# A new order of 36 transfers, and eleven instead of seven pairs of x tiles transposed on VectorE

## The chip, the cores and the metric

The kernel runs on one core of one Trainium2 chip. The metric is device microseconds of one execution. A profiled execution also has a *span*, from the first to the last instruction, some 2 us shorter than the time. Most executions of the kernel before agree within 0.3%. In the lines of the profile PE is TensorE, DVE is VectorE, ACT is ScalarE, and SPq is the sequencer that issues all transfers.

## The reference

```python
# x (16, 512, 1024), weight (1024, 768), sub_value (16, 512, 768), all float32
def reference(x, weight, sub_value):
    return (np.matmul(x, weight) - sub_value).astype(np.float32)
```

The rows of x form 64 tiles of 128 rows ("tile 0" to "tile 63"). x is 33.6 MB, the weight 3.1, sub_value and the output 25.2 each: 87.0 MB that any kernel has to move.

## The kernel before

Each x tile is cast to float16 on ScalarE. It is then transposed, either on TensorE (PE: four transposes and a copy on ScalarE) or, in pairs of tiles listed in `ON_DVE`, on VectorE. PE multiplies, and VectorE subtracts sub_value from the product in PSUM, the memory into which PE writes. One queue issues all transfers in the order of a list; `(kind, first tile, count)`.

```python
ON_DVE = frozenset(range(18, 60, 6))          # 7 pairs
TRANSFERS = [
    ('x', 0, 1), ('w', 0, 1), ('x', 1, 1), ('w', 1, 1), ('x', 2, 1), ('w', 2, 1),
    ('w', 3, 1), ('x', 3, 2), ('s', 0, 1), ('x', 5, 3), ('s', 1, 3), ('x', 8, 3),
    ('s', 4, 4), ('x', 11, 5), ('s', 8, 8), ('x', 16, 8), ('x', 24, 3), ('s', 16, 8),
    ('x', 27, 5), ('o', 0, 8), ('s', 24, 8), ('x', 32, 8), ('s', 32, 8), ('o', 8, 8),
    ...
]
```

x lives in a ring of 16 tiles, sub and out share a ring of 32. A transfer is not issued before its ring slots are free, and nothing behind it in the list is issued before it:

```python
need, by = {
    "w": (set(), "o"),
    "x": ({t for t in old if t >= 0}, "cast"),    # tiles 16 back are cast
    "s": ({t for t in old if t >= 0}, "o"),       # outputs 32 back are written
    "o": (span, "finish"),                        # these tiles are subtracted
}[kind]
if not need <= done[by]:
    return
```

Inside an iteration of the main loop (tile `mi`), PE multiplies tile `mi` with the transposes of tile `mi + 2` in between; then come the casts of tiles ahead (4 ahead for PE's tiles, 7 for VectorE's), the subtraction, and four of the 16 transposes of a pair on VectorE.

Of the kernel before, what the change touches and what calls it, by code (L numbers as in the profile page):

```python
# [17 lines left out]
LEAD_DVE = 7  # L18
PER = 4
HEAD = 3  # L20
ON_DVE = frozenset(range(18, 60, 6))

TRANSFERS = [
    ('x', 0, 1), ('w', 0, 1), ('x', 1, 1), ('w', 1, 1), ('x', 2, 1), ('w', 2, 1),
    ('w', 3, 1), ('x', 3, 2), ('s', 0, 1), ('x', 5, 3), ('s', 1, 3), ('x', 8, 3),
    ('s', 4, 4), ('x', 11, 5), ('s', 8, 8), ('x', 16, 8), ('x', 24, 3), ('s', 16, 8),
    ('x', 27, 5), ('o', 0, 8), ('s', 24, 8), ('x', 32, 8), ('s', 32, 8), ('o', 8, 8),
    ('x', 40, 8), ('s', 40, 8), ('x', 48, 8), ('o', 16, 8), ('o', 24, 8), ('s', 48, 8),
    ('x', 56, 8), ('s', 56, 8), ('o', 32, 8), ('o', 40, 8), ('o', 48, 8), ('o', 56, 4),
    ('o', 60, 2), ('o', 62, 1), ('o', 63, 1),  # L30
]


# [1 line left out]
def kernel(  # L35
# [88 lines left out]
    def cast(mi):  # L124
        assert mi in done["x"]
        done["cast"].add(mi)
        x_in = x_ring[:, mi % NX]
        first = mi - mi % 2
        if first in ON_DVE:
            if mi == first:  # L130
                x16_t["pair", mi] = x16p_pool.tile([P, 2, K], F16, name="x16p_tile")
            keep(nc.scalar.copy(out=x16_t["pair", first][:, mi - first], in_=x_in))  # L132
        else:
            x16_t[mi] = x16_pool.tile([P, K], F16, name="x16_tile")
            keep(nc.scalar.copy(out=x16_t[mi], in_=x_in))  # L135
        issue()


    def transposes(mi):
        def one(c):  # L140
            def f():
                if c == 0:
                    ps_t[mi] = psum_t_pool.tile([P, K], F16, name="psum_t")
                keep(nc.tensor.transpose(  # L144
                    ps_t[mi].bitcast(F32)[:, c * P : (c + 1) * P],
                    x16_t[mi].bitcast(F32)[:, c * P : (c + 1) * P],
                    ident,
                ))
                if c == n_c - 1:
                    xt_t[mi] = xt_pool.tile([P, K], F16, name="xt_tile")  # L150
                    keep(nc.scalar.copy(out=xt_t[mi], in_=ps_t.pop(mi)))  # L151
                    x16_t.pop(mi)
            return f
        return [one(c) for c in range(n_c)]

    def transposes_dve(mi):

        x16 = x16_t.pop(("pair", mi)).bitcast(F32).rearrange("p j (c q) -> p (j c) q", c=n_c)
        xt_p = xtp_pool.tile([P, 2, K], F16, name="xtp_tile")
        xt_t[mi], xt_t[mi + 1] = xt_p[:, 0], xt_p[:, 1]  # L160
        xt = xt_p.bitcast(F32).rearrange("p j (c m) -> p (j c) m", c=n_c)

        def one(a, b):
            def f():
                keep(nc.vector.transpose(  # L165
                    xt[b * Q : (b + 1) * Q, :, a * Q : (a + 1) * Q],
                    x16[a * Q : (a + 1) * Q, :, b * Q : (b + 1) * Q],
                ))
            return f
        return [one(a, b) for a in range(P // Q) for b in range(P // Q)]  # L170
# [14 lines left out]
    def finish(mi):  # L185
        assert mi in done["s"]
        done["finish"].add(mi)
        o = so_ring[:, mi % NSO].rearrange("p (h n) -> p h n", h=2)
        keep(nc.vector.tensor_tensor(  # L189
            out=o, in0=po_t.pop(mi)[:, :, :NS], in1=o, op=mybir.AluOpType.subtract  # L190
        ))
        issue()
# [10 lines left out]
    def idle(n):  # L203
        for _ in range(n):
            keep(nc.tensor.matmul(idle_o[:, 0], idle_w, idle_x, start=True, stop=True))  # L205

    def lead(mi):
        return LEAD_DVE if mi - mi % 2 in ON_DVE else TA + CA

# [1 line left out]
        for f in transposes(mi):  # L211
            f()

    idle(13)
    cast(0)
    transpose_tile(0)
    idle(5)
# [28 lines left out]
    for mi in range(HEAD, n_mt):  # L246
        t = mi + TA
        tr = transposes(t) if t < n_mt and t - t % 2 not in ON_DVE else []
        for c in range(n_c):
# [6 lines left out]
        finish(mi)  # L256
        if mi + LEAD_DVE - 1 in ON_DVE:
            waiting += transposes_dve(mi + LEAD_DVE - 1)
# [34 lines left out]
```

## Time and profile before

| | before |
|---|---|
| time, median of the first three runs | 211.42 us |
| span of the profiled run | 209.4 us |
| DMA queue, share of 16 engines' span | 97.7% |
| PE / VectorE / ScalarE busy | 198.4 / 114.1 / 112.6 us |
| last subtraction starts | 204.5 us |

The lines that carry these stand in the prediction. One more view: the queue's own issues in order of time (start, length, what, count).

```profile
78.97 0.33 SPq L122 DMA_DIRECT2D x_ring<-in_x_dram  x1
80.94 0.33 SPq L122 DMA_DIRECT2D so_ring<-in_sub_value_dram  x1
81.32 0.42 SPq L120 DMA_DIRECT2D out_dram<-so_ring  x1
```

The first line is the issue of x 32-39. At that moment the end of outputs 0-7 and all of sub 24-31 were still queued ahead of it.

### The profile page before, as it was taken

What the parts mean: (1) busy time and instruction counts of PE and PEld (TensorE: products, weight loads), DVE (VectorE), ACT (ScalarE), POOL (GpSimd) and SP (SyncE); (2) the same over time, 40 slices, a digit from 0 to 9 for tenths busy, and PEclk for the clock granted to TensorE, in tenths of its full rate; (3) what the DMA queues carried; (4) which work ended last, traced back from release to release, by engine and by line L of the source; (5) the groups of instructions that cost most, each with busy time, mean ns of one, the idle gap of its engine ahead of it and who ended that gap; (6) DMA issues with size and microseconds to landing.
All of it is one profiled execution on the core that took longest, in us unless ns stands there. A gap on an engine that the chain in (4) does not pass through costs nothing.

```text
span 209.4 us, 2967 instructions
## 1 busy us (share of the span) xinstructions
PE 198.4 (95%) x1249; PEld 130.4 (62%) x1249; DVE 114.1 (54%) x186; ACT 112.6 (54%) x115; POOL 0.7 (0%) x6
## 2 busy tenths in 40 slices
PE   7998789999979999999999999999999999999990
PEld 2464467676656576676666666667666766766660
DVE  0342044206149849929946965992994795332231
ACT  3555565675396183655727629355573760765410
POOL 1000000000000000000000000000000000000000
PEclk9999999999999999999999999999999999999999
DMA  6999999999999999999999999999999999999994
GB/s 221 420 426 424 424 438 439 433 443 426 391 455 415 442 427 423 454 413 432 435 421 449 423 413 444 451 418 421 418 441 440 423 437 418 426 446 427 415 383 167
DMA packets 5629, 87.22 MB, mean 417 GB/s; under 512 B 624, under 2 KB 624, under 8 KB 2032
## 3 DMA queue, kind: packets, MB, share of 16 engines
q1 hardware_dynamic: 5616, 87.03, 97.7%
q8 instruction: 10, 0.16, 0.3%
q14 instruction: 3, 0.02, 0.0%
HBM read 61.87 MB, written 25.17 MB: 416 GB/s over the span
## 4 chain that ended last, share of the span: by engine, by line
PE 68%; DMA 20%; ACT 4%; DVE 3%; SPq 1%; issue 1%
PE psum_o L177 60%; DMA x_ring<-in_x_dram 20%; PE psum_t L144 8%; ACT x_tile L135 2%; DVE xtp_tile L165 2%; ACT xt_tile L151 1%; DVE so_ring L189 1%; SPq L110 1%; SPq L122 1%; ACT x16p_tile L132 0%
## 5 line engine op out<-in xcount | busy, mean ns | idle before, releaser
L177 PE MATMUL psum_o<-w_sb,xt_tile 128*128 128x384 f16 x800 | 145.7, 326 | 1.7 <-ACT xt_tile L151 1.1
L177 PEld LDWEIGHTS <-xt_tile 128*128 128x128 f16 x800 | 78.2, 98 | 41.5 <-ACT xt_tile L151 1.9
L189 DVE TENSOR_TENSOR so_ring<-psum_o,so_ring 128x768 f32<-128x768 f32 x64 | 60.7, 957 | 61.2 <-PE psum_o L177 41.1
L151 ACT COPY xt_tile<-psum_t 128x1024 f16<-128x1024 f16 x50 | 50.6, 1012 | 75.7 <-PE psum_t L144 74.9
L165 DVE STREAM_TRANSPOSE xtp_tile<-x16p_tile 32x256 f32<-32x256 f32 x112 | 48.8, 436 | 18.9 <-ACT x16p_tile L132 17.2
L144 PE MATMUL psum_t<-ident,x_tile 128*128 128x128 f32 x200 | 52.5, 275 | 2.8 <-ACT x_tile L135 2.4
L135 ACT CAST x_tile<-x_ring 128x1024 f16<-128x1024 f32 x50 | 51.6, 1049 | 5.5 <-DMA x_ring<-in_x_dram 5.5
L177 PE MATMUL psum_o<-w_sb,xtp_tile 128*128 128x384 f16 x224 | 42.9, 326 | 0.3 <-DVE xtp_tile L165 0.3
L144 PEld LDWEIGHTS psum_t<-ident,x_tile 128*128 128x128 f32 x200 | 27.8, 142 | 16.8 <-ACT x_tile L135 4.7
L177 PEld LDWEIGHTS <-xtp_tile 128*128 128x128 f16 x224 | 21.8, 98 | 10.4 <-DVE xtp_tile L165 0.7
L132 ACT CAST x16p_tile<-x_ring 128x1024 f16<-128x1024 f32 x14 | 14.6, 1046 | 5.8 <-DMA x_ring<-in_x_dram 4.7
L205 PE MATMUL psum_o<-idle_x,idle_w 128*128 128x512 f16 x25 | 8.8, 508 | 1.3 <-DVE idle_x L200 1.3
L112 DVE CAST w_sb<-so_ring 128x768 f16<-128x768 f32 x8 | 4.1, 556 | 10.5 <-DMA so_ring<-in_weight_dram 10.5
L205 PEld LDWEIGHTS <-idle_w 128*128 128x128 f16 x25 | 3.0, 120 | 5.0 <-issue 3.2
L135 ACT ACT_TABLE_LOAD x1 | 1.3, 1283 | 0.7 <-PEq L277 0.7
L199 DVE MEMSET idle_w<- 128x64 uint32 x1 | 0.1, 112 | 0.8 <-PEq L277 0.8
masks.py:199 POOL TENSOR_SCALAR_AFFINE_SELECT ident<-ident 128x128 f32<-128x128 f32 x1 | 0.3, 292 | 0.1
L200 DVE MEMSET idle_x<- 128x256 uint32 x1 | 0.3, 272 | 0.0
masks.py:197 POOL MEMSET ident<- 128x128 f32 x1 | 0.2, 205 | 0.3 <-POOLq L277 0.3
L277 POOL MEMSET const-bfloat16-1.0<- 128x1 bf16 x1 | 0.1, 101 | 0.0
L277 POOL MEMSET const-uint8-127<- 128x1 uint8 x1 | 0.1, 101 | 0.0
L277 POOL MEMSET const-float32-0.0<- 128x1 f32 x1 | 0.1, 98 | 0.2 <-issue 0.2
(1 smaller groups left out, 0.1 us busy)
## 6 DMA issues: line engine op xcount, KB each, us to landing
so_ring<-in_sub_value_dram SPq DMA_DIRECT2D x7, 3072.0 KB, 24.2
out_dram<-so_ring SPq DMA_DIRECT2D x7, 3072.0 KB, 31.2
x_ring<-in_x_dram SPq DMA_DIRECT2D x5, 4096.0 KB, 22.3
x_ring<-in_x_dram SPq DMA_DIRECT2D x2, 2560.0 KB, 23.3
x_ring<-in_x_dram SPq DMA_DIRECT2D x3, 1536.0 KB, 19.8
so_ring<-in_weight_dram SPq DMA_DIRECT2D x4, 768.0 KB, 8.7
x_ring<-in_x_dram SPq DMA_DIRECT2D x3, 512.0 KB, 6.2
so_ring<-in_sub_value_dram SPq DMA_DIRECT2D x1, 1536.0 KB, 22.2
```

Of the source, the lines that this page charges most:

```text
L110: keep(nc.sync.dma_start(out=st, in_=w_c[at]))
L112: keep(nc.vector.tensor_copy(out=w_sb[:, at, r], in_=st[:, r]))
L122: keep(nc.sync.dma_start(out=here, in_=there))
L132: keep(nc.scalar.copy(out=x16_t["pair", first][:, mi - first], in_=x_in))
L135: keep(nc.scalar.copy(out=x16_t[mi], in_=x_in))
L144: keep(nc.tensor.transpose(ps_t[mi].bitcast(F32)[:, c * P : (c + 1) * P], x16_t[mi].bitcast(F32)[:, c * P : (c + 1) * P], ident,))
L151: keep(nc.scalar.copy(out=xt_t[mi], in_=ps_t.pop(mi)))
L165: keep(nc.vector.transpose(xt[b * Q : (b + 1) * Q, :, a * Q : (a + 1) * Q], x16[a * Q : (a + 1) * Q, :, b * Q : (b + 1) * Q],))
L177: keep(nc.tensor.matmul(po_t[mi][:, h, :NS], xt_t[mi][:, 2 * P * c + r : 2 * P * (c + 1) : 2], w_sb[:, c, r, h * NS : (h + 1) * NS], start ...
L189: keep(nc.vector.tensor_tensor(out=o, in0=po_t.pop(mi)[:, :, :NS], in1=o, op=mybir.AluOpType.subtract))
L205: keep(nc.tensor.matmul(idle_o[:, 0], idle_w, idle_x, start=True, stop=True))
L277: nc = _bacc.Bacc("TRN2", target_bir_lowering=False, num_devices=1)
```

## The change

It is meant to take PE's waits for x away: the weight comes first, x in larger pieces behind it, and four more pairs go to VectorE.

```diff
-ON_DVE = frozenset(range(18, 60, 6))
+ON_DVE = frozenset((12, 16, 20, 24, 28, 32, 38, 42, 46, 50, 54))
 TRANSFERS = [
-    ('x', 0, 1), ('w', 0, 1), ('x', 1, 1), ...
-    ('w', 3, 1), ('x', 3, 2), ('s', 0, 1), ('x', 5, 3), ('s', 1, 3), ('x', 8, 3),
-    ...('s', 16, 8),
-    ('x', 27, 5), ('o', 0, 8), ('s', 24, 8), ('x', 32, 8), ('s', 32, 8), ('o', 8, 8), ...
+    ('w', 0, 1), ('x', 0, 1), ('x', 1, 1), ...
+    ('w', 3, 1), ('x', 3, 4), ('s', 0, 4), ('x', 7, 1), ('x', 8, 8), ('s', 4, 4),
+    ('s', 8, 8), ('x', 16, 4), ('x', 20, 4), ('s', 16, 8), ('x', 24, 8), ('s', 24, 8),
+    ('x', 32, 8), ('o', 0, 8), ('o', 8, 8), ('s', 32, 8), ('x', 40, 8), ('s', 40, 8), ...
-    idle(13)
+    idle(16)          # idle matmuls ahead of the first tile
```

(The lists go on in the same manner.)

## The prediction

> **What bounds the kernel now.** I read the page's forty slices first, then its queue shares, then stage windows of the end, then the chain of waits, and last the cost rows.
>
> ```profile
> PE   7998789999979999999999999999999999999990
> GB/s 221 420 426 424 424 438 439 433 443 426 391 455 415 442 427 423 454 413 432 435 421 449 423 413 444 451 418 421 418 441 440 423 437 418 426 446 427 415 383 167
> q1 hardware_dynamic: 5616, 87.03, 97.7%
> ```
>
> Two things are full at once. TensorE (PE) is at 9 from slice 12 on, and the one DMA queue is busy 97.7% of 16 engines' span with 87.03 MB, a volume fixed by the reference. Only the first and the last two slices move clearly less than 400 GB/s. The windows of the end, two microseconds each (columns: PE, PE load, VectorE, ScalarE, GpSimd, then granted clock, DMA share, GB/s), show what is left there:
>
> ```profile
> 200.00:202.00 2.00, 2.00 (x14) 1.17 (x12) 0.25 (x2) 0.35 (x1) 0.00 (x0) 1.00 1.00 420
> 202.00:204.00 2.00, 2.00 (x15) 1.21 (x13) 0.84 (x1) 0.00 (x0) 0.00 (x0) 1.00 0.83 338
> 204.00:206.00 2.00, 0.45 (x3) 0.06 (x1) 0.96 (x1) 0.00 (x0) 0.00 (x0) 1.00 0.60 243
> 206.00:208.00 2.00, 0.00 (x0) 0.00 (x0) 0.00 (x0) 0.00 (x0) 0.00 (x0) 1.00 0.56 224
> ```
>
> After 202 us 2 x (338 + 243 + 224) KB = 1.61 MB are moved in a stretch in which PE has the last word. The two windows of 0 to 4 us move 0.62 MB (27 and 282 GB/s), so from 4 to 202 us it is 84.99 MB, or **429 GB/s**. At that rate 1.61 MB take 3.75 us instead of 6: a perfect queue would end about 2.2 us earlier. That is **all the DMA leaves to gain**: span about 207.2 us. The measured time is 2.0 us over the span (211.42 against 209.4), so the floor is about 209.2 us. The 2% line, 207.2 us, lies beneath it.
>
> The chain of waits has PE at 68% of the span and this at its start and end (start, length, what):
>
> ```profile
> 4.14 13.12 DMA x_ring<-in_x_dram
> ...
> 28.41 28.13 DMA x_ring<-in_x_dram
> ...
> 74.56 0.11 PE psum_t L144
> 74.67 0.65 PE psum_o L177 x4
> ...
> 199.25 5.21 PE psum_o L177 x32
> 204.49 0.96 DVE so_ring L189
> ```
>
> The reader should see two waits for x early, then unbroken matmuls. It also gives PE's true prices: four matmuls 0.65 us, a transpose slipped in behind them 0.11 us, so a tile costs 16 matmuls = 2.60 us, and 3.04 us with its four transposes.
>
> ```profile
> L189 DVE TENSOR_TENSOR so_ring<-psum_o,so_ring 128x768 f32<-128x768 f32 x64 | 60.7, 957 | 61.2 <-PE psum_o L177 41.1
> L165 DVE STREAM_TRANSPOSE xtp_tile<-x16p_tile 32x256 f32<-32x256 f32 x112 | 48.8, 436 | 18.9 <-ACT x16p_tile L132 17.2
> L144 PE MATMUL psum_t<-ident,x_tile 128*128 128x128 f32 x200 | 52.5, 275 | 2.8 <-ACT x_tile L135 2.4
> ```
>
> **What the Trainium skill says.** "TensorE: Matmul & The Clock Gate", Part 4: PE-mode transpose, gives about 275 ns in a kernel; row L144 agrees (275), but its price is the 0.11 us of the chain, since it overlaps. "Perfetto Trace Analysis", Identifying the Most-Contended Engine, warns that matmul busy time is a poor measure because of such pipelining; this trace agrees. "VectorE: DVE Perf Modes", The three transpose paths: VectorE transposes 32x32 blocks only; here that is 16 instructions for a pair of tiles, 436 ns each. "DMA: Bandwidth & Descriptors", Where 436 GB/s comes from, sets a fabric ceiling of 435 GB/s and says that HBM traffic binds at about 358; the trace's 429 exceeds the second and is close under the first, so I expect no faster stream.
>
> **The change part by part.**
>
> *Transposes.* Four more pairs go to VectorE: 8 tiles x 4 x 0.11 = **3.5 us off PE's path**. ScalarE loses 8 copies of 1.01 us. VectorE gains 64 x 0.436 = 27.9 us, to 142 us of 209. Total load is harmless, but from m tile 6 to 51 nearly every iteration holds a subtraction and four transposes. Before, such periods start 2.80 us apart (60.44, 63.24, 66.04); PE's mean iteration with half of the tiles transposed is (2.60 + 3.04) / 2 = 2.82. VectorE keeps pace with no reserve; three PSUM buffers and a two-iteration head start of each pair cover a lag of some 2 us.
>
> *Head.* I add up the bytes in order (x tile 0.524 MB, weight chunk 0.786, sub and out tiles 0.393) and turn them into landings: before, x tiles 3-4 complete 5.77 MB and land at 17.28 us, which is 5.77/0.429 + 3.8; x 16-23 complete 22.02 MB and land at 56.56, which is 5.2 over. The first matmul waits for w0 either way; x0 now lands second, at about 6.6 us instead of 4.72, so it starts 1 us later, but w3 and x3 gate what follows. x 3 now comes with 4 to 6: 6.82 MB, about 20.2 us instead of 17.28. **PE loses 2.9 us there**, less 0.6 that it waited for VectorE at tile 4, since sub 0-3 now comes in one early piece: +2.3.
>
> *x 8-15 and sub 4-7.* In one piece, x 8-15 lands at 13.11/0.429 + 5.2 = 35.7 us. PE reaches the transposes of x8, in iteration 6, at about 36.0: a wait of about 0.8 us. Tile 7 needs a PSUM buffer freed by tile 4, whose sub lands at 39.4: another 0.7.
>
> *Middle.* x 16-19 lands at 51.6, ahead of the long wait before (56.56). The 1.6 us that PE idled from 50 to 90 us before (18.78 and 19.66 busy of 20) go. x 20-23 (56.5), x 24-31 (73.6), x 40-47 (123), x 48-55 (147) and x 56-63 (165) each come before PE needs them, by my iteration count.
>
> Sum for PE: 204.5 + 2.3 + 1.5 - 3.5 - 1.6 = **203.2 us** for its end, 1.3 earlier.
>
> *DMA.* The count of bytes is the same; three transfers fewer is nothing. But the order has a thin place: x 32-39 directly follows sub 24-31, which ends at 32.51 MB, 75.7 + 2.9 = 78.6 us (2.9 is the lag of data behind bytes/0.429; 20.2 MB had moved at 50 us). x 32-39 may be issued once x 16-23 are cast. The built order of ScalarE puts the casts of 24, 22, 25, 23 in a row, and 24 lands at 73.6: 73.6 + 4 x 0.95 = 77.4. Issue to data takes some 1.5 us (the last 0.39 MB before: issue 205.5, landing 208.5, 0.9 of it data). So the queue **runs dry for about 0.5 us**; outputs 0-15, long ready, stand behind x in program order and cannot fill in. Before, the same issue at 78.97 had 7 us of work ahead of it.
>
> *Tail.* Sub 56-63 has only 24 output tiles behind it instead of 32. It lands at 77.60/0.429 + 5.2 + 0.5 = 186.5; PE starts tile 59, which needs tile 56 subtracted, at 189: no wait. Outputs 56-60 are issued near 196, 61-62 near 201.7, 63 near 204.2; the queue should be backed up until about 205.6, then the last piece runs with a landing near 208. Span about **208.6**, time 208.6 + 1.9 = **210.5 us**.
>
> **The rivals.** (1) *Full DMA gain*: no dry spot, backed up to the end: 209.2. For it: 97.7% share. Against: x 32-39 sits on a 1 us margin. (2) *The late head passes through*: if PE loses 2.3 + 1.5 early and VectorE, with no reserve, holds it back again, the 3.5 are eaten and PE ends near 205 or later, time 211.5 to 212.5. For it: the 2.80 against 2.82; against: PE's psum buffers, and VectorE's waits before were mostly for others (61.2 us ahead of L189). (3) *A chain of dry spots*: a late cast makes x 32-39 late, that makes x 40-47 late, and so on: each microsecond of empty queue is a microsecond of time, 212 to 214. For it: x goes out only after casts; against: out 0-15 queue behind it, 14.7 us of work.
>
> **Range and chances.** I choose 210.5: less than half of the 2.2 us that the DMA allows, because the dry spot and the last output's latency stay. The floor makes the lower end hard: 209.2. Upward I allow rival 2 in full and part of rival 3: 212.4. Faster by over 2% would need a rate above the 429 seen: 0.02. Slower by over 2% (215.6) needs several dry spots: 0.04. The rest is within 2%.
>
> **What would show it right or wrong.** Right: DMA share near 98% with no slice under 400 between the first and the last two; row L144 at 168, L165 at 176; PE's last matmul near 203; a PE wait ending with x3 near 20 us and one near x8 at 36; the issue of x 32-39 near 77.5 with a dip in GB/s at 79. Wrong: PE held repeatedly by VectorE's transposes or subtractions after 40 us (rival 2); several slices well under 400 GB/s (rival 3); or a middle rate far from 429, which would shift every landing.

## The result, and the profile after

| | before | changed |
|---|---|---|
| median of 6 runs | 211.22 us | 213.18 us (212.62 to 214.03) |
| span of the profiled run | 209.4 us | 211.0 us (its time 212.78) |
| last subtraction starts | 204.5 us | 203.65 us |

The ratio is 1.0096 (interval 1.0071 to 1.0121). Ratios here are the mean time of one kernel's fast runs over that of the other's of the same rounds, so not quite the ratio of the medians quoted. The change made the kernel about 1% slower. That is "within 2%", as forecast, but above the range of 209.2 to 212.4.

The forty slices and the queue share of the changed kernel:

```profile
PEclk9999699999999999999999999999999999999995
DMA  6999999999999998989999999999999999999993
GB/s 239 386 446 426 463 404 413 447 416 419 452 433 427 424 412 363 394 379 440 438 432 429 453 401 435 439 432 416 433 440 430 432 429 424 424 432 443 401 424 163
q1 hardware_dynamic: 5184, 87.03, 97.6%
```

Three slices in a row, 79 to 95 us, moved 363, 394 and 379 GB/s; before, no such group was there. In the same order of columns as the windows in the prediction, the stretch of 80 to 100 us, first before, then changed:

```profile
80.00:100.00 20.00, 20.00 (x131) 13.48 (x130) 15.27 (x28) 10.73 (x11) 0.00 (x0) 1.00 1.01 432
```

```profile
80.00:100.00 20.00, 20.00 (x129) 12.98 (x127) 19.39 (x37) 11.61 (x12) 0.00 (x0) 1.00 0.98 398
```

PE is busy all 20 us in both. The transfers lost (432 - 398) x 20 us = 0.68 MB, which is 1.6 us at 429 GB/s. In finer windows of the changed kernel the loss lies mostly from 86 to 92 us, well after the gap:

```profile
86.00:88.00 2.00, 2.00 (x14) 1.22 (x13) 1.94 (x4) 1.93 (x3) 0.00 (x0) 1.00 0.89 352
88.00:90.00 2.00, 2.00 (x15) 1.35 (x14) 1.93 (x6) 0.00 (x0) 0.00 (x0) 1.00 1.11 279
90.00:92.00 2.00, 2.00 (x15) 1.42 (x14) 1.94 (x4) 0.68 (x1) 0.00 (x0) 1.00 0.83 356
```

The chain of waits of the changed kernel shows what stood ahead of x 32-39:

```profile
55.41 18.52 DMA x_ring<-in_x_dram
...
74.03 1.04 ACT x16p_tile L131
75.08 0.95 ACT x_tile L134
76.02 0.95 ACT x16p_tile L131
76.97 0.95 ACT x_tile L134
...
77.94 0.33 SPq L121
```

x 24-31 lands at 73.93 us, ScalarE casts tiles 24, 22, 25, 23 one behind the other, and the last cast lets x 32-39 go at 77.94. Nothing else was left in the queue but the rest of sub 24-31.

What this place cost can be read from the landings. A transfer is spread over 16 DMA engines, and the trace has one completion for each of them. In the table below, worked out from these completions, "lag" is the landing of the slowest engine minus the bytes up to and with the transfer, divided by 429.2 KB per us. Where the queue keeps its rate the lag is level.

```
changed kernel         MB so far   first   median   last    lag
x 24-31                  29.36     71.30    71.69   73.93   5.52
sub 24-31                32.51     78.59    78.99   81.23   5.49
x 32-39                  36.70     90.58    90.92   92.52   7.01
out 63 (the last)        87.03    207.12   208.10  209.92   7.14
kernel before
sub 24-31                35.65     85.99    86.40   88.16   5.09
x 32-39                  39.85     95.70    96.33   97.88   5.04
out 63 (the last)        87.03    207.60   207.68  208.51   5.73
```

The lag grows by **1.52 us** at x 32-39 (2.16 on the median engine, whose landings are 11.93 us apart where 4.19 MB take 9.77) and stays. The last landing is 1.41 us later than before, the span 1.6 us longer.

In single packets of the trace: at 78.5 us half of the engines have nothing left, the first packets of x 32-39 start at 78.91 to 79.2, and 11 of the first 14 take 1.5 to 2.3 us, where a 32 KB row in a running stream takes 1.21. And once more, in the last rows of the same transfer: 18 rows that start between 86.8 and 89.9 us take 1.7 to 2.35 us. Averaged over the 16 engines that is 0.44 us of idle time, 0.48 us in the slow first rows and 1.06 us in the slow last ones, so the idle time is the smallest part. The slowest engine, whose landing the lag measures, had no gap at all: it ended sub 24-31 at 80.79 us and went straight on, six rows took 1.21 to 1.22 us, and the last two, from 88.07 us on, 1.82 and 2.29. All of its loss lies there. Why the last rows are slow no run shows.

What the prediction had right can be seen in these rows and waits of the changed kernel:

```profile
L164 DVE STREAM_TRANSPOSE xtp_tile<-x16p_tile 32x256 f32<-32x256 f32 x176 | 76.7, 436 | 7.6 <-ACT x16p_tile L131 4.9
L143 PE MATMUL psum_t<-ident,x_tile 128*128 128x128 f32 x168 | 43.8, 276 | 5.4 <-ACT x_tile L134 5.3
21.14 0.66 PE L143 MATMUL psum_t<-ident,x_tile 128*128 128x128 f32 x4 [3.08 <-ACT x_tile L134]
21.63 3.54 PE L176 MATMUL psum_o<-w_sb,xt_tile 128*128 128x384 f16 x12
189.14 0.81 PE L176 MATMUL psum_o<-w_sb,xt_tile 128*128 128x384 f16 x4 [0.63 <-DVE so_ring L188]
```

The four more pairs are there (176 and 168 instructions). PE waits 3.08 us for x 3, as the prediction's account of the head had it. After 40 us VectorE held PE back only once, by 0.63 us. New is the second PE line: 12 matmuls took 3.54 us there, and 2.11 us at the same place before. After the wait the clock granted to PE was at half for 3.4 us, the 6 in the PEclk row.

### The profile page after: what moved, and what is told of

It reads as the page before. It is cut to its first block, busy times and chain, and to the rows that moved or that the text cites. A ratio compares the mean times of both kernels' runs of the same rounds, so it can differ in the third digit from the quotient of the medians.

```text
span 211.0 us, 2956 instructions
## 1 busy us (share of the span) xinstructions
PE 195.9 (93%) x1220; PEld 126.8 (60%) x1220; DVE 141.3 (67%) x250; ACT 105.0 (50%) x107; POOL 0.7 (0%) x6
## 3 DMA queue, kind: packets, MB, share of 16 engines
q1 hardware_dynamic: 5184, 87.03, 97.6%
## 4 chain that ended last, share of the span: by engine, by line
DMA 82%; PE 7%; ACT 4%; SPq 3%; DVE 1%; issue 1%; ACTq 0%; DVEq 0%
DMA out_dram<-so_ring 44%; DMA x_ring<-in_x_dram 30%; DMA so_ring<-in_sub_value_dram 7%; PE psum_o L176 6%; ACT x_tile L134 2%; ACT x16p_tile L131 2%; SPq L121 1%; SPq L109 1%; DVE so_ring L188 1%; PE psum_t L143 1%; SPq L119 0%; ACTq L131 0%; DVEq L188 0%
## 5 line engine op out<-in xcount | busy, mean ns | idle before, releaser
L176 PE MATMUL psum_o<-w_sb,xt_tile 128*128 128x384 f16 x672 | 120.0, 329 | 1.0 <-DVE so_ring L188 1.0
L176 PEld LDWEIGHTS <-xt_tile 128*128 128x128 f16 x672 | 66.1, 99 | 39.0 <-issue 2.5
L150 ACT COPY xt_tile<-psum_t 128x1024 f16<-128x1024 f16 x42 | 42.5, 1012 | 79.4 <-PE psum_t L143 79.2
L164 DVE STREAM_TRANSPOSE xtp_tile<-x16p_tile 32x256 f32<-32x256 f32 x176 | 76.7, 436 | 7.6 <-ACT x16p_tile L131 4.9
L176 PE MATMUL psum_o<-w_sb,xtp_tile 128*128 128x384 f16 x352 | 67.4, 326 | 0.0
L143 PE MATMUL psum_t<-ident,x_tile 128*128 128x128 f32 x168 | 43.8, 276 | 5.4 <-ACT x_tile L134 5.3
L134 ACT CAST x_tile<-x_ring 128x1024 f16<-128x1024 f32 x42 | 43.6, 1046 | 9.8 <-DMA x_ring<-in_x_dram 9.8
L176 PEld LDWEIGHTS <-xtp_tile 128*128 128x128 f16 x352 | 34.4, 98 | 15.5 <-DVE xtp_tile L164 0.3
L143 PEld LDWEIGHTS psum_t<-ident,x_tile 128*128 128x128 f32 x168 | 23.4, 143 | 16.9 <-ACT x_tile L134 5.8
L131 ACT CAST x16p_tile<-x_ring 128x1024 f16<-128x1024 f32 x22 | 23.0, 1046 | 4.5 <-DMA x_ring<-in_x_dram 4.4
```

The lines of the kernel that those rows point to most:

```text
L131: keep(nc.scalar.copy(out=x16_t["pair", first][:, mi - first], in_=x_in))
L134: keep(nc.scalar.copy(out=x16_t[mi], in_=x_in))
L143: keep(nc.tensor.transpose(ps_t[mi].bitcast(F32)[:, c * P : (c + 1) * P], x16_t[mi].bitcast(F32)[:, c * P : (c + 1) * P], ident,))
L150: keep(nc.scalar.copy(out=xt_t[mi], in_=ps_t.pop(mi)))
L164: keep(nc.vector.transpose(xt[b * Q : (b + 1) * Q, :, a * Q : (a + 1) * Q], x16[a * Q : (a + 1) * Q, :, b * Q : (b + 1) * Q],))
L176: keep(nc.tensor.matmul(po_t[mi][:, h, :NS], xt_t[mi][:, 2 * P * c + r : 2 * P * (c + 1) : 2], w_sb[:, c, r, h * NS : (h + 1) * NS], start ...
```

## The experiments

Two questions were open: what made the changed kernel slower, and why did PE's earlier end buy nothing. Kernels of one call were timed on one chip beside the kernel before, whose median lay between 211.08 and 211.21 in every call. The changed kernel was not timed again, so a comparison with its 213.18 goes through the kernel before.

| run | median us | ratio to before (interval) |
|---|---|---|
| outputs 0-7 ahead of x 32-39 (changed kernel) | 211.43 | 1.0017 (0.9997 to 1.0038) |
| the dry place made in the kernel before | 220.15 | 1.0419 (1.0397 to 1.0442) |
| half the matmuls, changed kernel | 212.43 | 1.0070 (1.0054 to 1.0086) |
| x 24-31 cut in two (changed kernel) | 212.76 | 1.0080 (1.0063 to 1.0096) |
| x 3 alone (changed kernel) | 213.44 | 1.0104 (1.0063 to 1.0146) |
| seven pairs in the changed kernel | 221.37 | 1.0492 (1.0460 to 1.0524) |
| eleven pairs in the kernel before | 210.98 | 0.9998 (0.9986 to 1.0011) |
| half the matmuls, kernel before | 209.87 | 0.9942 (0.9929 to 0.9954) |
| short matmuls, kernel before | 211.02 | 1.0001 (0.9987 to 1.0014) |
| more fetches, kernel before | 211.48 | 1.0011 (0.9996 to 1.0026) |
| outputs first and x 3 alone (changed kernel) | 210.92 | 0.9997 (0.9984 to 1.0011) |

### Is it the dry queue?

**Outputs 0-7 ahead of x 32-39**, in the changed kernel:

```diff
-    ('x', 32, 8), ('o', 0, 8), ('o', 8, 8),
+    ('o', 0, 8), ('x', 32, 8), ('o', 8, 8),
```

> The changed kernel with one move: the transfer of outputs 0-7 stands ahead of x 32-39 instead of behind it, so that the queue has 7.3 us of work while the casts are awaited. Theory (the queue ran dry at 78 us and that alone made the changed kernel slow): the landing of x 32-39 no longer falls 1.5 us further behind its bytes, GB/s between 80 and 100 us comes back from 398 to about 430, time 211.2 to 211.7, so 1.5 to 2.0 us under the changed kernel's 213.18 and level with the kernel before. Rival of the prediction (a full queue could end at 209.2): 209.2 to 210.0. Rival (the loss lies in the late head, the clock dip or VectorE): stays near 213.

The result was 211.43 us. x 32-39 was issued at 78.20, even later than in the changed kernel, but with outputs 0-7 in the queue, and the stretch of 80 to 100 us is full again:

```profile
80.00:100.00 20.00, 20.00 (x129) 12.97 (x128) 18.86 (x36) 9.30 (x10) 0.00 (x0) 1.00 1.01 431
```

The lag goes from 5.74 to 5.59 across outputs 0-7 and x 32-39. One swap in the list takes the loss away, the slow rows with it: over all rows of x 32-39 they are 0.06 us per engine above 1.21 us a row, against 1.54 in the changed kernel. It does not bring the 209.2 of a "full queue".

**The dry place made in the kernel before:**

```diff
-    ('x', 27, 5), ('o', 0, 8), ('s', 24, 8), ('x', 32, 8), ('s', 32, 8), ('o', 8, 8),
+    ('x', 27, 5), ('s', 24, 8), ('x', 32, 8), ('o', 0, 8), ('s', 32, 8), ('o', 8, 8),
```

> The kernel before with one move: outputs 0-7 and sub 24-31 change so that x 32-39 directly follows sub 24-31, as in the changed kernel; transposes, head and all else as before. Theory (a dry queue at that place is the cost): x 32-39 is issued near 79 us with nothing before it in the queue, the lag of landings behind bytes grows by 1.5 to 2.2 us there, time 212.8 to 213.6 against 211.2. Rival (VectorE's and the head's load made the changed kernel slow): stays at 211.2 to 211.5.

The direction was right, the size was missed by far: 220.15 us. The lag grew by 3.7 us at x 32-39 (5.21 to 8.91) and by another 4.9 at sub 32-39 (to 13.78). I had overlooked the second one. Sub 32-39 takes the slots of outputs 0-7 and is issued only after they have landed (101.7 us), and in this order outputs 8-15 stand behind it, so the queue was empty meanwhile. This run shows that such a place costs time with seven pairs and the old head too; it gives no size for the changed kernel's.

**Half the matmuls, changed kernel** (one of the two halves of K left out, the result wrong):

```diff
-        for r in range(2):
+        for r in range(1):
...
-                    stop=(c == n_c - 1 and r == 1),
+                    stop=(c == n_c - 1),
```

> The changed kernel with half of its matmuls left out (wrong on purpose). Theory (the issue of x 32-39 waits for casts that wait for the landing of x 24-31, so the dry queue is made by the order alone, whatever PE does): the lag still grows by 1.2 to 2 us at x 32-39 and the time stays at 212.3 to 213.3. Rival (PE's late head and VectorE's lack of reserve delay the casts): dry spot gone, 211 or under.

212.43 us; x 32-39 was issued at 78.03 (77.94 in the changed kernel) and the lag grew by 1.88. A PE with half of its work does not fill the gap. With eleven pairs the casts wait for x 24-31, not for PE. (This run also has fewer instruction fetches, 5 instead of 9, which matter below; so the 0.75 us under the changed kernel is not clearly PE's.)

**x 24-31 cut in two**, a smaller dose:

```diff
-    ('x', 24, 8),
+    ('x', 24, 2), ('x', 26, 6),
```

> The changed kernel with x 24-31 cut into x 24-25 and x 26-31, so that the casts of 24 and 25, which stand ahead of that of 23, need not wait for all eight tiles. A smaller dose of the dry spot: ScalarE is free for them at 72.9 us instead of 74.0, so x 32-39 is issued near 76.8 instead of 77.9, 1.1 us earlier. If each microsecond of dry queue is a microsecond of time: lag growth at x 32-39 of 0.2 to 0.8 instead of 1.5, time 211.8 to 212.4. If the dry spot is not the cause: 213.

The issue moved as foreseen (76.94 us), and the median engine lost 1.05 us at x 32-39 instead of 2.16. The slowest engine's lag grew all the same, by 1.75 us, and the time was 212.76: outside the expected 211.8 to 212.4, nearer to the 213 expected if the dry spot is not the cause, and not clear of the changed kernel (ratios 1.0080 and 1.0096, with intervals that overlap). So a microsecond of earlier issue is not a microsecond of time. The packets say why: the engines were idle for less than 0.05 us on average, so the queue hardly ran dry, and yet the first rows were slow (up to 1.8 us) and 19 of the later ones too (up to 2.9 us). In all six runs in which x 32-39 came to a queue that held nothing but, at most, the rest of sub 24-31 (the changed kernel, this run, half the matmuls in the changed kernel, x 3 alone, seven pairs, and the dry place in the kernel before), the rows of x 32-39 took 1.5 to 2.1 us per engine more than 1.21 us each, whether the engines had been idle for less than 0.05 us or for 3.7 us just before; in the kernel before and the two runs with the outputs first it was 0.04 to 0.06 us. What the order costs in the changed kernel is thus mostly slow rows, not idle engines.

**x 3 alone**, to take the late head away:

```diff
-    ('w', 3, 1), ('x', 3, 4), ...
+    ('w', 3, 1), ('x', 3, 1), ('x', 4, 3), ...
```

> The changed kernel with x 3 in a transfer of its own ahead of x 4-6, nothing else. Theory (with eleven pairs the casts before x 32-39 wait for the landing of x 24-31, not for PE): the 3.1 us wait of PE for x 3 and most of the half clock go, x 32-39 is still issued within 0.5 us of 77.9, the lag still grows by 1.2 us or more there, time 212.5 to 213.3. Rival (the late head carries through): 211.5 or under.

213.44 us (212.19 to 214.23), just above the expected range. The head is not what costs. The expectation was wrong in two parts: x 32-39 was issued at 78.54, a little more than the allowed 0.5 us late, and the wait moved on. PE no longer waits 3.1 us for x 3, but 3.4 us for PSUM, as sub 0-3 was still to land, and the half clock came again.

```profile
21.71 0.66 PE L143 MATMUL psum_t<-ident,x_tile 128*128 128x128 f32 x4 [1.14 <-ACT x_tile L134]
25.77 1.41 PE L176 MATMUL psum_o<-w_sb,xt_tile 128*128 128x384 f16 x4 [3.40 <-DVE so_ring L188]
```

**Seven pairs in the changed kernel:**

```diff
-ON_DVE = frozenset((12, 16, 20, 24, 28, 32, 38, 42, 46, 50, 54))
+ON_DVE = frozenset(range(18, 60, 6))
```

> The changed kernel with the seven pairs of the kernel before; order and head as changed. Prediction's account (3.5 us off PE's path): 215 to 216.5, that is 2 to 3 us over the changed kernel. Theory (the queue sets the end and goes dry by its order, PE has about 2 us to spare): 213.0 to 214.0, the lag at x 32-39 again 1.5 us or more, PE's last matmul near 206.5.

Both expectations were wrong: 221.37 us. The issues of x 32-39 and what follows:

```profile
81.46 0.33 SPq L121 DMA_DIRECT2D x_ring<-in_x_dram  x1
81.88 0.86 SPq L119 DMA_DIRECT2D out_dram<-so_ring  x2
103.82 0.34 SPq L121 DMA_DIRECT2D so_ring<-in_sub_value_dram  x1
```

With more tiles transposed on PE, the casts stand behind more copies that wait for PE, and x 32-39 is issued 3.5 us later than with eleven pairs. The lag grew by 5.2 us there, by 2 more at x 56-63, and on to 15.0. So the two halves of the change belong together: this order is bearable only with pairs that let ScalarE run ahead. The pairs are worth 8 us in it. Most of that came through the time at which x is issued; but PE ended late as well (the last output is issued at 215.44, and all 16 engines land it within 0.22 us), and in the last transfers the lag still rose by 1.4 us. How the 8 us divide was not tested.

### Was there anything to gain?

**Eleven pairs in the kernel before**, its order kept:

```diff
-ON_DVE = frozenset(range(18, 60, 6))
+ON_DVE = frozenset(range(18, 60, 4))
```

> The kernel before with eleven pairs on VectorE (first tiles 18, 22, ... 58) and nothing else changed: order of transfers and head as before. The prediction valued the four further pairs at 3.5 us off PE's path with 2.2 us of it to be had, which makes 209.2 to 209.8. Theory (the end is set by the fullest DMA engine, which is backed up whatever PE does): PE's last matmul near 201 to 202 instead of 204.5, the last landing within 0.6 us of 208.5, time 210.7 to 211.2.

The last subtraction came 3.0 us earlier than before:

```profile
201.49 0.96 DVE L189 TENSOR_TENSOR so_ring<-psum_o,so_ring 128x768 f32<-128x768 f32 x1 [1.64 <-PE psum_o L177]
```

The time is 210.98 us, ratio 0.9998. So the 3 us off PE's path are real and buy nothing: the last landing moved from 208.51 to 208.31.

**Half the matmuls, kernel before** (the same edit as above):

> The kernel before with half of its matmuls left out (one of two interleaved halves of K; the result is wrong on purpose), all transfers as before. PE then has 8 instead of 16 matmuls a tile and waits for data. Prediction's floor (the last 1.6 MB moved slowly because PE came last, 2.2 us to be had): 209.0 to 209.6. Theory (one of the 16 DMA engines is backed up from start to end and sets the last landing, so PE was never the bound of the end): 210.4 to 211.3, the last transfer landing within 0.5 us of where it did before (208.5).

209.87 us, between the two expectations and nearer to the prediction's. Taken alone it says that PE had been in the way after all. But a kernel with half of the matmuls also has a shorter program, and the program comes through the same DMA engines. The page's instruction queue, kernel before and then this run (packets, MB, share):

```profile
q8 instruction: 10, 0.16, 0.3%
```

```profile
q8 instruction: 6, 0.10, 0.2%
```

**Short matmuls, kernel before:** as light a PE with as long a program.

```diff
-                    po_t[mi][:, h, :NS],
+                    po_t[mi][:, h, : NS if r == 0 else Q],
...
-                    w_sb[:, c, r, h * NS : (h + 1) * NS],
+                    w_sb[:, c, r, h * NS : h * NS + (NS if r == 0 else Q)],
```

> As the half-matmul run of the kernel before (209.87 us), but no instruction is left out: every second pair of matmuls is cut to 32 of 384 columns (wrong on purpose). PE is as light, its program as long, so as many 16 KB instruction fetches (10 against 6) cross the DMA engines. If the gain of the half-matmul run came from PE getting out of the way: again 209.6 to 210.1. If it came from fewer fetches on the fullest engine: 210.6 to 211.2, with a jump of about 1 us in the lag of landings after a fetch near 180 us.

211.02 us, ratio 1.0001. With PE done 12 us earlier than in the kernel before (the last subtraction starts at 192.16) the time is the same to 0.1%. PE is not what sets the end; the gain of the half-matmul run came with the shorter program.

**More fetches:** nearly all matmuls short, and half of them issued twice.

```diff
-        for r in range(2):
+        for i, r in enumerate((0, 1, 1)):
...
-                    po_t[mi][:, h, :NS],
+                    po_t[mi][:, h, : NS if c == 0 and r == 0 else Q],
```

(and the same width for the weight, `start` and `stop` on the first and last pass)

> The kernel before with nearly all matmuls cut to 32 of 384 columns and half of them issued twice (wrong on purpose): PE's program has 3309 rows instead of 2285, so about 14 instruction fetches of 16 KB instead of 10 cross the DMA engines, while PE stays lighter than in the kernel before. If fetches on the fullest engine are what sets the end: 211.5 to 212.3, above the kernel before and above the run with short matmuls (211.02), with a further jump of about 1 us in the lag of landings. If the fetches are harmless: 209.8 to 211.1. If PE turns out to be slower than thought, the landing of outputs waits for subtractions, which the trace would show, and the run says nothing.

211.48 us, just under the expected 211.5 to 212.3. The medians lie in order, but in the ratio this run is not clear of the kernel before (1.0011, from 0.9996). The landings of the last transfer say more. In all four runs in which PE is out of the way at the end, the *emptiest* engine ends at the same time, and the *fullest* later with more fetches (9 and 10 are alike):

```
run                              fetches   first    median   last landing of out 63
half the matmuls                    6      204.84   206.06   207.05
eleven pairs in the kernel before   9      204.96   206.56   208.31
short matmuls                      10      204.71   206.60   208.26
more fetches                       14      204.96   207.06   208.96
kernel before (for comparison)     10      207.60   207.68   208.51
```

Each fetch is one packet of 16 KB and takes 0.9 to 1.1 us of one engine. In the kernel before, the lag of the fullest engine rises in two steps, from 3.90 to 5.08 in the transfer that lands after the fetch at 22.1 us, and from 4.48 to 5.68 after that at 182.7. In the table's last line most engines waited for PE's last tile (their landings bunch at 207.6); the fullest had no such gap and ended within 0.3 us of the run with a light PE and as many fetches. Which fetch goes to which engine I did not establish, so that the fetches set the end is likely and not shown.

**Both mends together** (outputs 0-7 first, x 3 alone), as a try to beat both kernels:

> The changed kernel with outputs 0-7 ahead of x 32-39 and x 3 in a transfer of its own ahead of x 4-6. Theory (only the dry queue cost time): the PE wait of 3.1 us for x 3 and the half clock after it go, PE ends about 2 us earlier than in the run with the outputs moved alone, yet the time stays at 211.0 to 211.4, level with the kernel before. Rival (PE's late head still cost something once the queue is full): 210.2 to 210.8, better than both kernels.

210.92 us against 211.08, ratio 0.9997: between the two expected ranges, better than the changed kernel, level with the kernel before. PE did not end earlier than with the outputs moved alone, against the expectation: the wait for x became one of 3.46 us for PSUM, and the half clock stayed. No version that beats both was found.

## Why the prediction was wrong

It missed by 2.7 us and in direction: 210.5 foretold, 213.18 measured, 211.2 before. By its own steps:

- **PE's path: right.** The sum gave 203.2 us for PE's end; it was 203.6. That it came so near is partly luck, as two of its terms were off and nearly cancelled: the head lost 1.4 us more, by the half clock, and the waits at x 8-15 and tile 7 came to 0.33 us instead of 1.5.
- **Landings: right.** x 3-6 at 20.2 (20.0), x 8-15 at 35.7 (35.2), x 24-31 at 73.6 (73.9). Sub 56-63 at 186.5 landed at 188.0; about 1.0 us of this is what the thin place had cost beyond the estimate. (The 84.99 MB behind the rate of 429 is reckoned from all 87.22 MB of the page, not from the queue's 87.03; the rate stays 428 to 429.)
- **"The queue runs dry for about 0.5 us": right place, mis-sized term.** The place cost 1.5 us on the slowest engine. The idle time, 0.44 us per engine, was about the 0.5 foretold, but by two errors that cancelled: the issue came at 77.94 instead of 77.4, and from there to the first packet it was 0.97 us instead of 1.5 (a figure that does not follow from the line it was taken from: 205.5 to 208.5, less 0.9, is 2.1). What stood in no term are the slow rows after it, 0.48 us per engine at the start of x 32-39 and 1.06 at its end; the slowest engine, never idle, lost its 1.5 us in the last two rows alone. The swap of one transfer gave 1.75 us back (213.18 to 211.43).
- **"A perfect queue would end about 2.2 us earlier. That is all the DMA leaves to gain": the step that was wrong in its mechanism.** I took the mean rate in the last 6 us as room that PE had left. It was the mean over 16 engines, most of them idle, and one that was never idle. A transfer lands with its fullest engine. Two runs show that PE did not hold this room: PE done 3 us earlier gave 210.98 us, PE done 12 us earlier gave 211.02; only a shorter program, in a third, gave 209.87. About 0.9 us of gain was built on it.
- **Rivals.** Rival 2 (VectorE without reserve) fell: 0.63 us of waiting after 40 us, and that for sub 56-63. Rival 3, a chain of dry spots, did not come about in the changed kernel, as outputs 0-15 stood behind x 32-39; it did in two experiments (220.15 and 221.37). That its 212 to 214 holds the measured 213.18 is chance, and three slices under 400 GB/s, its sign, came from one place.

The term of the thin place (1.0 us too small) and the floor (0.9 us that was not there) explain 1.9 of the 2.7 us. Of the rest part is that the profiled run (212.78) was among the fastest of six. Why the changed kernel spreads over 1.4 us, the kernel before over 0.3, stays open: only one run has a trace. The thin place alone does not explain it: with the outputs moved ahead the spread was still 1.2 us (210.90 to 212.08).

## What to carry to other kernels

When one queue is nearly full, order its transfers so that something which needs no waiting stands ahead of each one that has to wait for an engine; here a transfer that met an empty or nearly empty queue cost 1.5 us and more, by idle engines and by slow rows at its start and end, and nothing later brought it back. Before counting the slack at the end as a gain, look at the slowest of the 16 DMA engines and not at their mean; the cheapest test is to make the other engine's work light, without shortening its program, and see whether the time moves. And test the parts of a change crosswise: four more pairs on VectorE were worth nothing in one order and 8 us in the other.

## What the Trainium skill lacked or had wrong

- "Runtime: NRT & Kernel Launch", Instruction fetch mechanics, has 16 KiB blocks of 256 instructions fetched by a queue of their own, the cost "mostly hidden". The blocks are as said (10 packets, 0.16 MB), and no wait of PE is put down to them. But each takes 0.9 to 1.1 us of one of the engines that move the data: in a kernel with a full queue, 6, 10 and 14 fetches went with last landings at 207.05, 208.26 and 208.96 us.
- "DMA: Bandwidth & Descriptors", Where 436 GB/s comes from, says that for transfers between HBM and SBUF about 358 GB/s binds. One core alone moved 429 GB/s from 4 to 202 us; the 435 of the fabric is the figure that fits. (A note above it on the same page gives 358 for two cores that stream at once; the sentence should say so.)
- The same page, Why a DMA increments its semaphore by 16 and not by 1, says that the engines finish independently; how far apart is on no page. Here it was up to 4.0 us (204.96 to 208.96).
- On no page: slow rows in a transfer that meets an empty or nearly empty queue: in the changed kernel 1.5 to 2.3 us for 11 of the first 14 rows of 32 KB instead of 1.21, and 1.7 to 2.35 us for 18 rows at its end, 8 to 11 us later.
- "TensorE: Matmul & The Clock Gate", Part 4: PE-mode transpose, gives about 275 ns (276 here), but not what it adds between matmuls, 0.11 us. The row "Avoid throughput drops mid-kernel" in its section Why this matters for your kernels agrees: after waits of 3.08 and 3.40 us PE ran at half clock for 3.4 us.
